# A two-layer denoiser block with an mLSTM layer: the decay rows reach all partitions by DMA and are masked by a select on GpSimd, not by two matmuls a direction, and the written-out orders of the instructions are new

## The chip, the cores and the metric

The kernel runs on one core of one Trainium2 chip. A core has five engines, each with an instruction queue of its own: TensorE (PE in the profile) multiplies matrices, VectorE (DVE) and ScalarE (ACT) work on rows of elements, GpSimd (POOL) does the same and here also starts some transfers, and SyncE (SP) starts most transfers. Each engine works off its queue in order. An instruction that waits for another engine, or for a transfer (DMA), holds up whatever stands behind it on its own queue. SBUF is the memory on the chip with 128 partitions, PSUM the small memory that TensorE writes into.

The metric is the device time of one execution in microseconds (us).

## What is computed

Input are 512 tokens of 1024 features (the latents), 256 tokens of context, and a conditioning vector. Two layers follow one another. Each normalises its tokens, scales and shifts them by the conditioning, mixes them, projects, and adds the result to the tokens with a gate. Layer 0 mixes by a long convolution (hyena) beside attention; layer 1 by an mLSTM, a linear recurrence with 8 heads (key size 128, value size 256) that runs over the tokens forwards and backwards. The change is in layer 1. Its reference, cut to what matters:

```python
def mlstm_chunkwise(q, k, v, i_pre, f_pre, state):        # chunks of the sequence
    def step(carry, inp):
        C, nvec, m = carry
        qc, kc, vc, ic, lfc = inp
        b = jnp.cumsum(lfc, axis=-1)
        d = jnp.where(lower, b[..., :, None] - b[..., None, :] + ic[..., None, :], -jnp.inf)
        inter = b + m[..., None]
        m_row = jnp.maximum(inter, jnp.max(d, axis=-1))
        s = jnp.einsum('bhtd,bhsd->bhts', qc, kc) * jnp.exp(d - m_row[..., None])
        w_prev = jnp.exp(inter - m_row)
        num = jnp.einsum('bhts,bhsv->bhtv', s, vc) + w_prev[..., None] * jnp.einsum('bhvd,bhtd->bhtv', C, qc)
        ...
st_f, hc_f = mlstm_chunkwise(qc, kc, vc, gc[0], gc[1], zero)
_, hl_f = mlstm_chunkwise(ql, kl, vl, gl[0], gl[1], st_f)
...  # and the same with everything flipped, for the backward direction
```

The kernel uses chunks of 128 tokens. With u = i - b and c the running maximum of u (and of the state that enters), the factor exp(d - m_row) for a token t and an earlier token s of the same chunk becomes exp(u[s] - c[t]), and 0 where s comes after t. In the kernel a tile E holds this factor with s along the partitions and t along the row, for the four chunks of the latents side by side: 128 x 512. So E needs, in all 128 partitions, the same row of -c (a row of 512 for each head and direction), a triangle of -1e30 on top of it (the mask), and u[s] as a bias of each partition.

## The kernel before

Everything is in float32, multiplied in pieces: each operand is split into a high and a low part (the function split, L1024: a cast on ScalarE, then a subtraction on VectorE), and a product takes three matmuls (mm3, L1034: high x high, high x low, low x high). Weights come in slices of 1024 x 256 (load_w, L1041): two transfers of 512 KB on SP's queue into tiles wr, each split into a half of a tile wh (ScalarE) and of wl (VectorE). There are 148 such halves. The tokens of a layer, normalised and transposed, lie split in hTh and hTl. Their way there: x_norm (L1144) makes xn, TensorE turns it, h_tile (L1154) scales and splits it.

The order of the instructions is written out by hand, for each part of the kernel. While a part is being recorded (record, L1009), no instruction is issued: an Engine object notes it down. play (L1014) then issues the notes in the order of a list of numbers in the table ORDERS (from L163), and each engine keeps that order. A second table, SLOTS, says for each tag of a pool which of its buffers each new tile takes. There are seven parts: start, hy (hyena), att (attention), out0 (output projection of layer 0 and the first token tiles of layer 1), l1a (first projections and the gates of layer 1), l1b (the eight heads), out1 (output projection of layer 1). Since all instructions are issued by play, the profile gives line L1019 for nearly all of them, and groups are told apart by the names of their tiles.

Layer 1 (from L2209), in the parts that the change and the prediction touch:

- gates (L2228) computes the gates of all heads and both directions at once, rows 0 to 7 forwards and 32 to 39 backwards. It uses ScalarE and VectorE for the most part, with some memsets of POOL ahead of it (gwh, gwl, onesf, gf, gi, q1, q2, zero, ncf, ncs). It leaves cq1 (columns with u and the factors of the keys), cq2, apb, and in ncf the rows of -c. ncf is split into ncs, whose rows 0 to 39 hold the high and rows 64 to 103 the low parts. pick is the sum of two pieces of an identity, so that a column of it, repeated 128 times, picks one row's high and low part and adds them.
- head (L2352) makes keys, queries and values of a head by projections, with short convolutions, then the gates so and zs, and the recurrence (from L2442). psS holds the four products of keys and queries of the chunks. For each direction d the exponent is put together in PSUM by two matmuls of 512 columns: pick's column times ncs writes the row of -c into all 128 partitions, and an identity (identr) times the table mask adds the triangle. ScalarE takes the exponential of it, chunk by chunk, with u as the bias:

```python
TE.matmul(pef, pick[:, col:col + 1].broadcast_to([P, P]), ncs, start=True, stop=False)   # L2452
TE.matmul(pef, identr, mask[:, d], start=False, stop=True)                               # L2453
E = T(mr, "E", (P, 4, P))
for n in range(4):
    S.activation(E[:, n], pe[:, n], AF.Exp, bias=cq1[:, n, col:col + 1])
V.scalar_tensor_tensor(E, psS, QS * KS, E, ALU.mult, ALU.mult)
```

- E is split (Eh, El). The keys, scaled by their factors (ka), are split (kah, kal). For six chunks the state C is updated from a matmul of kah with the values (vh, vl), and num, the result of each chunk, takes a part from Eh and a part from C. Between the steps stand pieces of the projections of so and zs.
- normed divides num by dn, weights it by so, normalises it (hss on ScalarE, hst on VectorE, hrs, a power, on POOL) and multiplies it by zs into hh; result turns hh by TensorE and writes it to DRAM. Both belong to the work left over to the next head. After the last head they stand ahead of out1.

Before the change identr (64 KB) and mask (512 KB) were loaded by POOL's queue at the start of l1a.

Of the kernel before, what the change touches and what calls it, by code (L numbers as in the profile page):

```python
# [7 lines left out]
F32 = mybir.dt.float32  # L8
# [6 lines left out]
P = 128  # L15
# [8 lines left out]
def _hilo(a):  # L24
    """float64 -> two float32 arrays of 12-bit significands whose sum carries 24 bits."""
# [11 lines left out]
def _tables():  # L37
# [8 lines left out]
    s_, t_ = np.arange(P)[:, None], np.arange(P)[None, :]  # L46
    mf = np.where(s_ <= t_, 0.0, -1e30).astype(f32)
    mb = np.where(s_ >= t_, 0.0, -1e30).astype(f32)
    t["mask"] = np.stack([np.tile(mf, (1, 4)), np.tile(mb, (1, 4))], 1)
    # rotary tables  # L50
# [9 lines left out]
    # hyena positional features, decays and transform matrices, tokens ordered phase by phase  # L60
# [27 lines left out]
def _cols(v):  # L88
    """[.., n*128] -> [128, n] columns"""
    v = np.asarray(v)  # L90
    return v.reshape(-1, P).T


def _layout(i):
    """inputs laid out for the device; values unchanged"""
# [58 lines left out]
# columns of vecs  # L154
# [3 lines left out]
class Ctx:  # L158
# [3 lines left out]
# the order in which the instructions noted down in a part of the kernel are issued  # L162
# [2485 lines left out]
```

## Time and profile before

| what | us |
| --- | --- |
| median of 3 runs | 1537.01 |
| lowest and highest of them | 1536.03, 1537.13 |
| span of the profiled execution, first to last instruction | 1533.4 |
| TensorE busy in it | 1499.6 |
| VectorE, ScalarE, GpSimd busy | 988.5, 716.9, 51.7 |

The profiled execution has no total of its own beside its span; the median of the runs is 3.6 us above that span, which is what lies around the first and the last instruction. In the page each engine has its busy time, its share of the span and the number of its instructions. PE's matmuls overlap: the next begins before the one before has ended, so durations of neighbours may not be added. In a row of a timeline stand start, duration, engine, line, operation, the tile written and the tiles read, and in brackets the time for which the engine sat idle before and what ended that. In a row of the list of waits stand the engine and the tile that it was about to write, behind the arrow the engine and tile that it waited for, then the total, the number of times and the longest. In a row of a window stand its length, and for each engine the busy time and in brackets the instructions, then the clock that the throttle granted to TensorE (1.00 is all of it), and the share and rate of the DMA engines.

### The profile page before, as it was taken

Reading aid. Unit: us, or ns where it says so; the run is one execution under the profiler, and the core shown is the slowest. Engines: PE = TensorE matmul, PEld = TensorE weight load, DVE = VectorE, ACT = ScalarE, POOL = GpSimd, SP = SyncE. Lnnn points to the kernel's source line nnn. Section 1 sums busy time; section 2 is a strip of 40 time slices with the busy share of each in tenths; the row PEclk is TensorE's granted clock in tenths of the full one; section 3 lists DMA queues with packets and bytes.
Section 4 is the critical chain, followed back from the end, with each engine's and each line's share of the span. In section 5 each row is a group of like instructions: output and inputs, shape, how many; then the busy total and the mean of one; then the engine's idle time right before and its main releaser. Section 6 shows DMA issues by size and latency. Waiting matters only on the chain.

```text
span 1533.4 us, 26152 instructions
## 1 busy us (share of the span) xinstructions
PE 1499.6 (98%) x10652; PEld 1380.3 (90%) x10652; DVE 988.5 (64%) x1947; ACT 716.9 (47%) x1554; POOL 51.7 (3%) x93
## 2 busy tenths in 40 slices
PE   7999999999999999999999899999999999999997
PEld 4889999889999999989988789999999999999885
DVE  6688786877866666684237755665656565666435
ACT  6643444434435454463225566545545453545332
POOL 1000000000000000000001200000000000000000
PEclk9999999999999999999999999999999999999999
DMA  9421211221130111443442402211221232213741
GB/s 375 138 71 51 78 65 51 71 72 39 40 122 29 38 67 61 156 141 105 175 168 97 147 28 87 67 58 63 97 73 56 73 97 73 70 66 104 257 168 69
DMA packets 42625, 148.13 MB, mean 97 GB/s; under 512 B 4928, under 2 KB 7625, under 8 KB 39946
## 3 DMA queue, kind: packets, MB, share of 16 engines
q1 hardware_dynamic: 38968, 137.12, 25.9%
q0 software_dynamic: 1648, 7.01, 1.4%
q10 hardware_dynamic: 1890, 2.34, 0.5%
q8 instruction: 84, 1.38, 0.3%
q14 instruction: 35, 0.29, 0.1%
HBM read 131.77 MB, written 14.68 MB: 96 GB/s over the span
## 4 chain that ended last, share of the span: by engine, by line
PE 93%; ACT 2%; DVE 2%; issue 1%; DMA 1%; SPq 0%; POOL 0%; POOLq 0%; DVEq 0%; ACTq 0%
PE pj L1019 77%; PE pm L1019 14%; PE s L1019 2%; ACT wh L1019 1%; DMA dfb<-y_scratch 1%; DMA xt<-in_x 0%; DVE wl L1019 0%; DVE hTl L1019 0%; ACT hf L1019 0%; ACT hTh L1019 0%; ACT q L1019 0%; DVE hf L1019 0%; DVE xn L1019 0%; DVE xnT L1019 0%; SPq L1019 0%
## 5 line engine op out<-in xcount | busy, mean ns | idle before, releaser
L1019 PE MATMUL pj<-wh,hTh 128*128 128x256 f32 (+1 forms) x1536 | 442.9, 289 | 3.3 <-ACT wh L1019 3.0
L1019 PE MATMUL pj<-wl,hTh 128*128 128x256 f32 (+1 forms) x1536 | 438.3, 285 | 3.2 <-DVE wl L1019 2.1
L1019 PE MATMUL pj<-wh,hTl 128*128 128x256 f32 (+1 forms) x1536 | 437.8, 285 | 0.0
L1019 PEld LDWEIGHTS pj<-wh,hTh 128*128 128x128 f32 x1536 | 290.0, 189 | 9.4 <-ACT wh L1019 4.3
L1019 PEld LDWEIGHTS pj<-wl,hTh 128*128 128x128 f32 x1536 | 291.5, 190 | 6.6 <-DVE wl L1019 4.3
L1019 PEld LDWEIGHTS pj<-wh,hTl 128*128 128x128 f32 x1536 | 290.9, 189 | 1.4
L1019 PE MATMUL pj<-hTh,wh 128*128 128x512 f32 (+1 forms) x832 | 287.1, 345 | 0.0
L1019 PE MATMUL pj<-hTh,wl 128*128 128x512 f32 (+1 forms) x832 | 285.3, 343 | 0.5 <-DVE wl L1019 0.5
L1019 PE MATMUL pj<-hTl,wh 128*128 128x512 f32 (+1 forms) x832 | 285.3, 343 | 0.5 <-DVE hTl L1019 0.5
L1019 DVE TENSOR_TENSOR wl<-wr,wh 128x1024 fp32r<-128x1024 f32 x148 | 180.1, 1218 | 77.4 <-ACT wh L1019 77.1
L1019 ACT CAST wh<-wr 128x1024 fp32r<-128x1024 f32 x148 | 154.1, 1049 | 72.4 <-PE pj L1019 49.3
L1019 PEld LDWEIGHTS pj<-hTh,wl 128*128 128x128 f32 x832 | 156.7, 188 | 21.2 <-DVE wl L1019 0.9
L1019 PEld LDWEIGHTS pj<-hTh,wh 128*128 128x128 f32 x832 | 156.8, 188 | 19.2 <-issue 0.8
L1019 PEld LDWEIGHTS pj<-hTl,wh 128*128 128x128 f32 x832 | 156.8, 188 | 19.0 <-DVE hTl L1019 0.8
L1019 DVE TENSOR_TENSOR PTl<-pj,PTh 128x384 fp32r<-128x384 f32 (+1 forms) x80 | 40.9, 523 | 21.5 <-ACT PTh L1019 21.4
L1019 ACT CAST PTh<-pj 128x384 fp32r<-128x384 f32 (+1 forms) x80 | 35.1, 459 | 40.9 <-PE pj L1019 38.5
L1019 DVE SCALAR_TENSOR_TENSOR C<-C,apb,pj 128x258 f32<-128x258 f32 x64 | 30.6, 479 | 31.2 <-PE pj L1019 30.2
L1019 DVE TENSOR_TENSOR Cl<-C,Ch 128x258 fp32r<-128x258 f32 x64 | 26.8, 423 | 37.1 <-ACT Ch L1019 36.8
L1019 DVE SCALAR_TENSOR_TENSOR num<-pm,cq,num 128x258 f32<-128x258 f32 x64 | 30.2, 480 | 25.4 <-PE pm L1019 10.9
L1019 PE MATMUL pm<-Rh,dfa 128*128 128x256 f32 (+1 forms) x192 | 44.7, 304 | 0.0
L1019 DVE TENSOR_REDUCE mx<-s 128x1 f32<-128x768 f32 (+1 forms) x48 | 36.9, 771 | 11.2 <-PE s L1019 11.2
L1019 DVE TENSOR_TENSOR med<-big 128x512 f32<-128x512 f32 (+1 forms) x48 | 40.4, 864 | 4.8 <-ACT big L1019 4.6
(341 smaller groups left out, 2725.3 us busy)
## 6 DMA issues: line engine op xcount, KB each, us to landing
wr<-in_o_w_in SPq DMA_DIRECT2D x64, 512.0 KB
wr<-in_e_w_in SPq DMA_DIRECT2D x52, 512.0 KB
wh<-in_w_mod SPq DMA_DIRECT2D x18, 1024.0 KB
wr<-in_e_w_out SPq DMA_DIRECT2D x16, 512.0 KB
wr<-in_o_w_out SPq DMA_DIRECT2D x16, 512.0 KB
xt<-in_x SPq DMA_DIRECT2D x12, 512.0 KB
y_scratch<-y SPq DMA_DIRECT2D x8, 512.0 KB
xt<-in_w_mod SPq DMA_DIRECT2D x6, 512.0 KB
```

The lines of the kernel that those rows point to most:

```text
L1019: x = fn(*a, **k)
```

## The change

The row of -c goes through DRAM. The two blocks of 8 rows of ncf are written to a scratch tensor in DRAM, by two transfers on SP's queue. For each head and direction a transfer on SP's queue reads one row (2 KB) into all 128 partitions of a tile decay (256 KB, two buffers). A select on POOL (affine_select) then puts -1e30 in place of the elements behind the diagonal, for the forward or the backward direction. Exp reads that tile in SBUF. Gone are the 32 matmuls and their 16 tiles of PSUM; the table mask, the loads of mask and identr; ncs with its memset, its split and the tile pick; and the memset of ncf.

```diff
-    identr = T(mg, "identr", (P, P), F32R)
-    G.dma_start(identr, ins["ident"])
-    mask = T(mg, "mask", (P, 2, 512), F32R)
-    G.dma_start(mask, ins["mask"])
...
-    ncs = T(mg, "ncs", (P, NL), F32R)  # rows of -c, high parts and low parts
-    pick = T(mg, "pick", (P, 40), F32R)  # columns that add both parts of a row
+    ncd = nc.dram_tensor("nc_scratch", [2, 8, NL], F32).ap()
...
-        G.memset(f(ncs), 0.0)
-        V.tensor_tensor(pick, ident[:, 0:40], ident[:, 64:104], ALU.add)
         ncf = T(gp, "ncf", (NR, NL))
-        G.memset(ncf, 0.0)
...
-        split(ncs[0:NR], ncs[64:64 + NR], ncf)
+        for d in range(2):
+            SP.dma_start(ncd[d], ncf[32 * d:32 * d + 8])
...
+        decay = []
+        for d in range(2):
+            x = T(mr, "decay", (P, 4, P), bufs=2)
+            SP.dma_start(x, ncd[d, h:h + 1].rearrange("o (n t) -> o n t", n=4).broadcast_to([P, 4, P]))
+            G.affine_select(x, x, [[0, 4], [1 - 2 * d, P]], ALU.is_ge, -1e30, base=0, channel_multiplier=2 * d - 1)
+            decay.append(x)
         psS = PM((P, 4, P))
...
-            pe = PM((P, 4, P))
-            pef = pe.rearrange("p n t -> p (n t)")
-            TE.matmul(pef, pick[:, col:col + 1].broadcast_to([P, P]), ncs, start=True, stop=False)
-            TE.matmul(pef, identr, mask[:, d], start=False, stop=True)
...
-                S.activation(E[:, n], pe[:, n], AF.Exp, bias=cq1[:, n, col:col + 1])
+                S.activation(E[:, n], decay[d][:, n], AF.Exp, bias=cq1[:, n, col:col + 1])
```

The second half of the change are the tables. All lists of ORDERS and most of SLOTS are new, of the parts too whose work stays the same. In "start" each engine keeps its order, and only the order of the issue across engines differs. In hy, att, out0, l1a, l1b and out1 the lists of TensorE, VectorE, ScalarE and SP differ; a TensorE instruction stands on average 22 to 33 places from where it stood, GpSimd's order is nearly as before. In the new lists of TensorE the matmuls of several PSUM tiles alternate more finely, where before a tile's matmuls stood in long runs. The buffers of wr, which were taken in turn (0, 2, 1), are now taken irregularly: 20 times of 148 a half takes the buffer of the half just before it, 14 times before. In l1b the new order has the reads of decay on SP among the loads of weights, and the selects on POOL among the memsets and powers. Comments are gone as well, with no effect on the instructions.

More of the change, by code (lines that the diff above doesn't have):

```diff
@@ L45, in _tables @@
     t["sel"] = sel
[L46 to L49, printed above, removed]
     nf = 32
@@ L808 @@
     "qTh@6": [
-        0, 0, 2, 1, 0, 2, 1, 0, 2,
+        0, 0, 1, 2, 0, 1, 2, 0, 1,
     ],
@@ L869 @@
     "xn@9": [
-        0, 2, 1, 0, 2, 1, 0, 2, 1, 0, 2, 1,
+        0, 1, 1, 2, 0, 2, 1, 0, 2, 1, 0, 1,
     ],
@@ L878 @@
     "cvo@12": [
-        0, 1, 1, 0, 1, 0, 1, 0, 1, 0, 1, 0, 1, 0, 1, 0, 1, 0,
+        0, 1, 0, 1, 1, 0, 0, 1, 1, 0, 1, 0, 0, 1, 0, 1, 1, 0,
     ],
     "vh@12": [
-        0, 1, 0, 1, 0, 1, 0, 1, 0,
+        0, 1, 0, 0, 1, 1, 0, 1, 0,
     ],
     "vl@12": [
-        0, 1, 0, 1, 0, 1, 0, 1, 0,
+        0, 0, 1, 0, 1, 0, 1, 1, 0,
     ],
     "hn@12": [
-        0, 1, 0, 1, 0, 1, 0, 1,
+        0, 1, 0, 1, 0, 0, 1, 0,
+    ],
+    "decay@13": [
+        0, 1, 0, 1, 0, 1, 0, 1, 0, 1, 0, 1, 0, 1, 0, 1,
@@ L907 @@
     ],
     "ess@14": [
-        0, 1, 0, 1,
+        1, 1, 1, 1,
     ],
     "esst@14": [
-        0, 1, 0, 1,
+        1, 0, 1, 0,
     ],
     "ers@14": [
-        0, 1, 0, 1,
+        1, 0, 1, 0,
     ],
     "xt@14": [
-        0, 3, 2, 1,
+        3, 0, 2, 1,
     ],
```

55 lines of the change are left out of this document (29 added, 26 removed), and 1162 rows, old and new, of tables (ORDERS, SLOTS).

## The prediction

> **What bounds the kernel now.** I read the page's first and fourth part first, the engines' busy time and the chain that ended last.
>
> ```profile
> span 1533.4 us, 26152 instructions
> PE 1499.6 (98%) x10652; PEld 1380.3 (90%) x10652; DVE 988.5 (64%) x1947; ACT 716.9 (47%) x1554; POOL 51.7 (3%) x93
> PE 93%; ACT 2%; DVE 2%; issue 1%; DMA 1%; SPq 0%; POOL 0%; POOLq 0%; DVEq 0%; ACTq 0%
> ```
>
> TensorE (PE) is busy 98% of the span, and 93% of the chain is its own work. So a matmul taken away shortens the kernel by its own pace, unless a wait fills the hole. The second view is a table by windows of 20 us: four places where PE is not full, and for comparison one from the middle of the heads (940 to 960).
>
> ```profile
> core 0: us, PE busy (x) PEld busy (x) DVE busy (x) ACT busy (x) POOL busy (x), PEclk, DMA share, GB/s
> 840.00:860.00 20.00, 16.75 (x87) 13.62 (x87) 17.19 (x41) 12.37 (x26) 3.05 (x5) 0.95 0.31 116
> 860.00:880.00 20.00, 17.16 (x106) 15.63 (x106) 16.44 (x27) 10.77 (x22) 8.30 (x17) 0.88 0.54 169
> 900.00:920.00 20.00, 17.69 (x140) 16.55 (x138) 14.63 (x38) 18.71 (x33) 0.00 (x0) 1.00 0.01 2
> 940.00:960.00 20.00, 20.00 (x122) 17.74 (x121) 13.94 (x29) 9.81 (x22) 0.37 (x6) 1.00 0.30 103
> 1420.00:1440.00 20.00, 16.80 (x131) 14.91 (x130) 10.55 (x20) 7.27 (x19) 1.05 (x1) 0.95 0.57 206
> ```
>
> Between 840 and 880, where layer 0's output projection hands tokens to layer 1, PE idles 3.25 + 2.84 = 6.1 us, and the granted clock falls to 0.95 and 0.88: (0.05 + 0.12) x 20 = 3.4 us of clock. 900 to 920 (the gates, ScalarE busy 18.7 of 20) idles 2.3 us; 1420 to 1440 (last head, start of the last projection) idles 3.2 us and loses another 1.0 by its clock. Among the heads PE is busy 20.00 of 20.00. The list of PE's waits says what ended these gaps:
>
> ```profile
> PE pj L1019 <- DMA fw<-in_f_w: 8.0, 1, 8.0
> PE pm L1019 <- DVE xn L1019: 4.1, 4, 1.8
> PE pj L1019 <- ACT wh L1019: 3.0, 3, 1.2
> PE pj L1019 <- DVE wl L1019: 2.5, 5, 0.7
> PE pm L1019 <- DVE hh L1019: 1.2, 1, 1.2
> ```
>
> The 8.0 us are the start and stay. None names a tile of the masks. All waits below the first come to little more than 10 us, so the new orders have little to win and a full PE to spoil.
>
> **Matmuls removed.** The timeline at the first mask of head 0:
>
> ```profile
> 929.61 0.28 PE L1019 MATMUL pj<-vh,kal 128*128 128x258 f32 x1
> 929.72 0.40 PE L1019 MATMUL pm<-ncs,pick 128*128 128x512 f32 x1
> 929.96 0.39 PE L1019 MATMUL pm<-mask,identr 128*128 128x512 f32 x1
> 930.18 0.28 PE L1019 MATMUL pj<-vh,kah 128*128 128x258 f32 x1
> 930.38 0.88 ACT L1019 ACTIVATE E<-pm,cq 128x128 f32<-128x128 f32 x3
> ```
>
> Matmuls overlap, so the price is start to start: 930.18 - 929.72 = 0.46 us for the pair. The groups count the pairs:
>
> ```profile
> L1019 PE MATMUL pm<-ncs,pick 128*128 128x512 f32 x16 | 6.4, 398 | 0.0
> L1019 PE MATMUL pm<-mask,identr 128*128 128x512 f32 x16 | 6.3, 394 | 0.0
> L1019 ACT ACTIVATE E<-pm,cq 128x128 f32<-128x128 f32 x64 | 21.0, 369 | 9.6 <-PE pm L1019 9.4
> ```
>
> 16 x 0.46 = **7.4 us**, all in the full stage, neither matmul with idle time before it. By the durations (6.4 + 6.3) it would be 12.7, which counts the overlap twice. The Trainium skill, "TensorE: Matmul & The Clock Gate", Part 1, puts a 512-column matmul at 215.7 ns start to start, by which the term would be an estimated 6.9; the trace shows 0.23. Exp (0.37 us) now reads SBUF, not PSUM; what that does to its duration falls on an engine that idles half of 940 to 960 (9.81 busy), so nothing of it is on the path.
>
> **Setup removed.** The timeline of GpSimd (POOL) and VectorE (DVE) where the last token tiles are normalised:
>
> ```profile
> 840.61 0.87 DVE L1019 TENSOR_SCALAR xn<-xt,rs 128x512 f32<-128x512 f32 x2
> 865.31 4.08 DVE L1019 TENSOR_SCALAR xn<-xt,rs 128x512 f32<-128x512 f32 x2
> 863.92 0.96 POOL L1019 MEMSET gwh<- 128x1024 f32 x1
> 867.75 0.59 POOL L1019 DMA_DIRECT2D identr<-in_ident  x1
> 868.84 0.67 POOL L1019 DMA_DIRECT2D mask<-in_mask  x1
> 869.50 0.54 POOL L1019 MEMSET ncf<- 40x512 f32 x1
> 868.24 0.63 PE L1019 MATMUL pm<-c_ident,xn 128*128 128x128 f32 x4 [1.80 <-DVE xn L1019]
> ```
>
> The same two operations took 0.87 us elsewhere and 4.08 while POOL ran its block of memsets and DMA issues from 863.9 to 870.0; PE waited 1.80 and then 0.58 us for xn. The change takes identr, mask and ncf out of that block, 1.8 us, but 3.2 us of slowing stays as long as the other memsets do. Gain between 0 and 1.8; I take **1.0**. The split of ncs goes too:
>
> ```profile
> L1019 ACT CAST ncs<-ncf x1: 618/618/618, 919.0 to 919.0; 40x512 fp32r<-40x512 f32 x1
> L1019 DVE TENSOR_TENSOR ncs<-ncf,ncs x1: 687/687/687, 920.3 to 920.3; 40x512 fp32r<-40x512 f32 x1
> L1019 POOL MEMSET ncs<- x1: 528/528/528, 874.6 to 874.6; 128x512 f32 x1
> ```
>
> 0.6 us of ScalarE where it is the busiest, 900 to 920: between 0 and 0.6; I take **0.5**.
>
> **Added: the row by DMA, the select, the wait of Exp.** Sixteen reads of 256 KB, broadcast to 128 partitions, on SP's queue, two small writes, and sixteen selects of 128x512 on POOL. No select is in the trace. The nearest rows:
>
> ```profile
> L1019 POOL TENSOR_TENSOR rq<-qst,mhalf 128x12 f32<-128x12 f32 x5 | 11.4, 2281 | 168.2 <-DVE qst L1019 168.2
> grow<-in_qk_norm POOLq DMA_DIRECT2D x2, 64.0 KB, 3.3
> mask<-in_mask POOLq DMA_DIRECT2D x1, 512.0 KB, 3.8
> identr<-in_ident POOLq DMA_DIRECT2D x1, 64.0 KB, 2.5
> SPq L1019 <- DVE wl L1019: 612.5, 62, 27.1
> L1019 DVE TENSOR_TENSOR wl<-wr,wh 128x1024 fp32r<-128x1024 f32 x148 | 180.1, 1218 | 77.4 <-ACT wh L1019 77.1
> ```
>
> One select costs between 0.53 (the memset of that size) and 2.3 us (the power); one pass over 512 elements, it is nearer to the memset than to a power; I take 1. POOL has 51.7 us of work in all, so 16 to 37 more fit. A read lands in 2.5 to 3.8 us by the DMA rows; 4 MB beside a DMA share of 0.30 fit too.
>
> On time they are by position. In the new order I add the PE work between a head's read on SP and its first Exp, at 0.12 us for a matmul of 256 columns (929.61 to 929.72 above) and 0.23 for 512. For heads 1, 2, 3, 4 and 7, first direction, it comes to 28, 20, 34, 47 and 20 us, for the second directions 21 to 43; need is 3.8 + 2.3 = 6.1. Tight are head 5 (read and Exp at the same point, though the SP instruction before it stands 11 us earlier, so the read may go out up to 11 us early if its buffer is free) and head 6 (its buffer comes free just before). SP waits mostly for wl (row above), so a read behind a blocked wr issue goes late with it. What a late Exp holds is ScalarE's queue: casts of wh and C behind it, and by those DVE's splits and PE. Head 0 has no lead: ncf on ScalarE, write, read, select, Exp in series, 2.5 + 3.3 + 1 = 6.8 us or up to 2.5 + 3.8 + 2.3 = 8.6; in before, ncs was ready at 920.3 + 0.7 = 921.0 and first used at 929.7, 8.7 us of slack. The new order has the first Exp 3 us of PE work earlier, which leaves 8.7 - 3 = 5.7 us for 6.8 to 8.6. So a wait of up to 3 us is possible there and the same at heads 5 and 6, nothing elsewhere: 0 to 9 us, of which ScalarE's own idle time (10 of 20 us in a window) covers most. I take **1.0** lost.
>
> **Orders anew.** The lists of PE, ScalarE, DVE and SP differ in hyena, attention, both projections and layer 1 (PE instructions move 22 to 33 places on average); "start" keeps the order of each engine. The work is the same; what can change are the gaps. Two can be followed:
>
> ```profile
> 1416.40 0.29 PE L1019 MATMUL pm<-Ch,ql 128*128 128x258 f32 x1
> 1424.30 1.56 PE L1019 MATMUL pm<-c_ident,hh 128*128 128x128 f32 x8 [1.25 <-DVE hh L1019]
> ```
>
> At the last head the chain from the last matmuls of num (a run that ends at 1416.5) to the transposes of hh takes 7.9 us, with 5.8 us of PE work in between; the new list puts 7.0 there: **1.2** gained. At the end of layer 0's projection the work between the last token tile's last matmul and its transposes falls from 8.2 to 6.8 us: up to 1.4 lost; I take **0.7**, as the xn gain above is at the same tile. Elsewhere there is little: of PE's idle 33.8 us (1533.4 - 1499.6) the start has 8.0 and the three places above 11.6; the other 14.2, the end of the kernel among them, lie in over 1400 us. I enter nothing and leave it to the range.
>
> Sum: -7.4 - 1.0 - 0.5 - 1.2 + 1.0 + 0.7 = -8.4. On the span: 1533.4 - 8.4 = 1525.0; the median of the runs is 3.6 us above the span, so **1528.6 us**.
>
> **Rivals.** (a) The new orders close the gaps. 6.1 + 3.4 us between 840 and 880, 2.3 at the gates, 4.2 at 1420 to 1440 are 16.0, of which my terms take 2.7 already; two thirds of the rest would be 9 more, about 1520. For it: the same work in better places would do it. Against: chains of ScalarE and DVE, not order alone, set these stages.
>
> (b) Slower: ScalarE's queue stands at Exp. Place: the first Exp of each direction; price: the time by which read and select come late. It decides when the 16 Exps hold PE for over 0.46 us each on average, since that is what a pair returned; at 1 us each the sum has +16 in place of +1.0, so -9.4 + 16 = 6.6 slower, about 1543.6. For it: SP's 612.5 us behind wl, and POOL's queue is in order, so a select behind a norm's power (hrs, which waits for DVE) waits with it. Against: the leads of 20 us and more.
>
> (c) DVE and POOL hold each other up: xn above took 4.08 for 0.87 us beside POOL. If each select held a DVE split by its own 1 to 2.3 us, DVE would lose 16 to 37 us over the 500 us of heads, where it has 6 of 20 idle; that costs PE only where wl (1.2 us a piece) is just in time, and at a tenth of it, 2 to 4 us, the time is about 1532. The Trainium skill, "SBUF — State Buffer", Who interferes with whom, says that a DVE instruction with two SBUF inputs contends with a GpSimd instruction that reads SBUF, not with one that only writes, and that the second fully blocks; by that rule a select, which reads, would hold the splits which are all such two-input forms. The trace has xn, one input, slowed by memsets, a form that the section lists as well; it has no select.
>
> (d) The new order of the full stages (hyena, attention, the heads) adds waits there that eat the matmuls' gain: eight heads with 1 us each are enough, about 1537. Nothing in the profile shows a gap that would grow, but at 98% any gap is new.
>
> (e) The pairs were not on the path: the change gives 0 to 2 us, about 1536. PE's 20.00 of 20.00 in 940 to 960 speaks against it.
>
> **Numbers.** Forecast 0.37 (its own range: all gains at their upper ends and no loss, 1526, to the matmuls alone with losses of 3 + 1.4, 1534); (a) 0.22; (c) 0.10; (d) 0.11 and (e) 0.04; (b) 0.16. A measurement of this kernel tells 0.2%, 3.1 us, from no change. Faster: forecast, (a), (c) and a little of (d), 0.70; same: the rest of (d) and (e), 0.14; slower: (b), 0.16. The range goes from (a) with all of the gaps closed, 1515, to (d) and the milder half of (b), 1541.
>
> **What would show it.** PE's count falls by 32 to 10620 and PE is still at 98%; the 20-us windows of the heads stay at 20.00; no wait named decay in ScalarE's list, or under 3 us in all; select rows on POOL at 0.5 to 2.3 us; hh's 1.25 gone; xn's waits under 4.1 in all; no window of the heads under a clock of 1.00. Wrong if ScalarE waits for decay and PE then for wh or C; if wl grows past 1218 ns on average; if half-clock stretches come or go (the one before 1440 cost 1.0 in its window); or if new waits stand in hyena and attention.

## The result

The changed kernel takes 1569.33 us (median of 4 runs, 1568.98 to 1572.72), the kernel before in the same comparison 1536.55 (1536.03 to 1537.13, 4 runs): a ratio of 1.0221 [1.0207, 1.0236], 32.8 us slower. The prediction said 1528.6 and at most 1541.

The profiled execution of the changed kernel took 1569.42 us with a span of 1567.4, 34.0 more than before. The same three lines of its page:

```profile
span 1567.4 us, 26209 instructions
PE 1523.5 (97%) x10620; PEld 1384.8 (88%) x10620; DVE 1016.4 (65%) x1945; ACT 728.9 (47%) x1553; POOL 60.4 (4%) x105
PE 37%; DVE 3%; ACT 1%; issue 0%; DMA 0%; POOL 0%; POOLq 0%; DVEq 0%; ACTq 0%
```

PE has the 32 matmuls less that were forecast (10620 for 10652) and is busy 23.9 us longer, at 97%. So most of the loss is not idle time: fewer matmuls cover more time. (The shares of the chain here come to 41%: it could not be followed through, and I don't use it.) The windows of 20 us, one from the first part of attention, two from layer 0's projection to layer 1, one of the heads, one at the last head:

```profile
core 0: us, PE busy (x) PEld busy (x) DVE busy (x) ACT busy (x) POOL busy (x), PEclk, DMA share, GB/s
440.00:460.00 20.00, 15.54 (x111) 14.79 (x110) 11.01 (x31) 8.09 (x32) 2.30 (x1) 0.87 0.28 82
880.00:900.00 20.00, 15.70 (x87) 13.40 (x85) 14.91 (x32) 10.92 (x22) 2.51 (x4) 0.83 0.22 78
900.00:920.00 20.00, 14.76 (x82) 13.31 (x83) 13.29 (x21) 8.68 (x18) 5.83 (x12) 0.83 0.43 131
980.00:1000.00 20.00, 20.00 (x125) 17.92 (x125) 15.31 (x32) 10.04 (x21) 0.00 (x0) 1.00 0.36 99
1455.00:1475.00 20.00, 17.44 (x149) 16.22 (x148) 10.08 (x18) 7.62 (x18) 1.01 (x1) 1.00 0.60 218
```

The heads are as full as they were. But 440 to 460, attention, idles 4.46 us at a clock of 0.87, and between 880 and 920 it is 4.30 + 5.24 = 9.5 us at 0.83, where before had 6.1 in its two windows. At the last head, which ends some 35 us later than in before, PE idles 2.56 us for 3.20, and its clock stays full. Both kernels issue a known number of matmuls in each part, so the matmuls can be counted off and the time from a part's first matmul to the next part's first can be read:

| part | before, us | after, us | difference |
| --- | --- | --- | --- |
| start | 43.1 | 43.4 | +0.2 |
| hy | 372.3 | 372.3 | 0.0 |
| att | 314.3 | 342.0 | +27.7 |
| out0 | 137.5 | 149.4 | +11.9 |
| l1a | 48.3 | 50.4 | +2.1 |
| l1b, the heads | 510.9 | 504.1 | -6.9 |
| out1 | 89.0 | 90.2 | +1.2 |

Of the +36 there go 0.5 at the first matmul and 1.9 behind the last one, which leaves the 34.0. The heads, where the masks were, gained 6.9. Attention, which the diff touches only by its order, lost four times as much. Read from the starts of the matmuls, the loss splits as follows. The runs of modulation matmuls, each from its first start to the start of the matmul behind it, take 19.3 us more (att 12.1, out0 5.0, out1 2.2). The matmul just ahead of a run mostly takes 0.2 to 0.3 us to the next start, not 0.12 (0.31 from 562.99 to 563.30 below), and there are 43 runs for 16, so about 4 us more belong to them (an estimate): some 23 in all. PE's idle time ahead of matmuls grows by 11.5 (att 7.4, out0 3.7, l1b 0.4). The removed matmuls give back 7.5, and the rest is mostly the clock: PE runs at half clock for 27.3 us (five stretches, from 454.9, 888.4, 905.5, 939.6 and 949.9), before for 10.2 (6.8 from 857.9 and 3.4 from 1438.2), without the stretch behind the last matmul that each kernel has.

**The modulation.** A modulation row (mod_row, L1107, called in att, out0 and out1) is eight matmuls with an output of 32 partitions each; k-tiles kt and kt + 4 use the same group of 32 columns of the array. In the profile they are the rows pj or pm <- wh,cond of 128*32, two records each. First before, by form, then after:

```profile
L1019 PE MATMUL pm<-wh,cond 128*32 128x256 f32 x160 | 10.7, 385 | 0.0
L1019 PE MATMUL pj<-wh,cond 128*32 128x256 f32 x128 | 8.6, 385 | 0.7 <-DVE dec L1019 0.7
```

```profile
L1021 PE MATMUL pj<-wh,cond 128*32 128x256 f32 x128 | 22.3, 387 | 0.0
L1021 PE MATMUL pm<-wh,cond 128*32 128x256 f32 x160 | 18.5, 386 | 0.2 <-issue 0.2
```

The mean of one is the same, 385 ns before, 387 and 386 after, and the busy time of the two groups grows by 13.7 + 7.8 = 21.5 us. So no matmul is slower, they overlap less. The timeline of PE at such a row, before and after:

```profile
589.41 1.07 PE L1019 MATMUL pj<-wh,cond 128*32 128x256 f32 x16
590.41 0.55 PE L1019 MATMUL pj<-c_ident,hdl 128*128 128x128 f32 x3
```

```profile
562.01 1.05 PE L1021 MATMUL pj<-wh,cond 128*32 128x256 f32 x4
562.99 0.38 PE L1021 MATMUL pj<-wh,hTl 128*128 128x256 f32 x1
563.30 0.62 PE L1021 MATMUL pj<-wh,cond 128*32 128x256 f32 x2
563.86 0.38 PE L1021 MATMUL s<-dfa,qTl 128*128 128x256 f32 x1
564.17 1.05 PE L1021 MATMUL pj<-wh,cond 128*32 128x256 f32 x4
565.15 0.39 PE L1021 MATMUL pj<-wl,hTh 128*128 128x256 f32 x1
```

Before, all 16 records stand in one run and pass in 590.41 - 589.41 = 1.00 us: the four column groups work side by side. After, four records alone take 562.99 - 562.01 = 0.98 us: they are kt and kt + 4 of one group and follow one another. Two records take 563.86 - 563.30 = 0.56. The Trainium skill, "TensorE: Matmul & The Clock Gate", Part 3, says that matmuls with outputs in different groups of 32 columns run at the same time; before's row agrees with it. The runs of both kernels follow one pattern, apart from three that hold a wait and one of 0.46 us: a run in which no group comes twice (1, 2 or 4 matmuls) takes 0.53 to 0.57 us, one in which a group comes twice (2 to 8 matmuls) 0.98 to 1.02. So what counts is into how many runs a row falls. In before each of the 16 rows of these three parts is one run; in after they stand in 2 to 5 runs (att), 1 to 3 (out0), 1 to 4 (out1).

**The waits.** PE's list, the costly rows and the one of hh:

```profile
PE pj L1021 <- DMA fw<-in_f_w: 7.5, 1, 7.5
PE pm L1021 <- ACT hf L1021: 6.0, 4, 2.7
PE pm L1021 <- DVE xn L1021: 4.2, 2, 3.4
PE pj L1021 <- ACT qjunk L1021: 4.2, 4, 2.8
...
PE pm L1021 <- DVE hh L1021: 1.3, 2, 0.8
```

hf and qjunk (the squares that the norm of queries and keys in attention needs) are new among the top rows; nothing here is decay.

### The profile page after: what moved, and what is told of

Read it like the earlier page. It is cut to its first block, busy times and chain, and to the rows that moved or that the text cites. A ratio compares the mean times of both kernels' runs of the same rounds, so it can differ in the third digit from the quotient of the medians.

```text
span 1567.4 us, 26209 instructions
## 1 busy us (share of the span) xinstructions
PE 1523.5 (97%) x10620; PEld 1384.8 (88%) x10620; DVE 1016.4 (65%) x1945; ACT 728.9 (47%) x1553; POOL 60.4 (4%) x105
## 3 DMA queue, kind: packets, MB, share of 16 engines
q1 hardware_dynamic: 41304, 141.35, 27.7%
## 5 line engine op out<-in xcount | busy, mean ns | idle before, releaser
L1021 PE MATMUL pj<-wh,hTh 128*128 128x256 f32 (+1 forms) x1536 | 426.4, 290 | 6.8 <-ACT wh L1021 2.1
L1021 PE MATMUL pj<-wl,hTh 128*128 128x256 f32 (+1 forms) x1536 | 429.7, 289 | 1.3 <-DVE wl L1021 1.3
L1021 PE MATMUL pj<-wh,hTl 128*128 128x256 f32 (+1 forms) x1536 | 426.0, 289 | 0.2 <-DVE hTl L1021 0.2
L1021 PE MATMUL pj<-hTh,wh 128*128 128x512 f32 (+1 forms) x832 | 282.3, 346 | 1.9 <-DVE qTl L1021 1.9
L1021 PE MATMUL pj<-hTl,wh 128*128 128x256 f32 (+1 forms) x832 | 282.7, 344 | 0.6 <-DVE hTl L1021 0.6
L1021 PE MATMUL pj<-hTh,wl 128*128 128x512 f32 (+1 forms) x832 | 280.0, 344 | 0.0
L1021 PE MATMUL s<-dfa,qTh 128*128 128x256 f32 (+1 forms) x160 | 45.8, 341 | 0.0
```

Source lines behind the costliest of these rows:

```text
L1021: x = fn(*a, **k)
```

## The experiments

Two theories to begin with. Mine after the result: the orders of the parts whose work did not change cost the time, first by the broken rows of the modulation, then by waits; the mask's change itself is worth about what was forecast. The rival: DMA reads, selects and what they hold up cost it, in the heads and ahead of them.

### First set: the mask or the orders

The kernel before took 1535.54 us (median of 15 runs) beside these four. **orders_alone** is the kernel before with the new tables:

```diff
-ORDERS = {"start": <before>, "hy": <before>, "att": <before>, "out0": <before>, "l1a": <before>, "l1b": <before>, "out1": <before>}
+ORDERS = {"start": <after>, "hy": <after>, "att": <after>, "out0": <after>, "l1a": <before>, "l1b": <before>, "out1": <after>}
```

> The kernel before (masks by two matmuls), with the new orders and buffers in start, hyena, attention and both output projections, those of before in l1a and l1b. Theory (orders outside layer 1 lose it): attention +28, first projection +12, last one +1: 1575 to 1580 us. Rival (the masks' new way loses it): within 5 us of before.

1578.24 us, 1.0273 [1.0259, 1.0287]. att +27.9, out0 +14.0, out1 +1.2, l1b 0.0. No select and no read of decay is in this kernel, and the loss is all there. The rival falls.

**mask_alone** is the changed kernel with the old tables outside layer 1's middle:

```diff
-ORDERS = {"start": <after>, "hy": <after>, "att": <after>, "out0": <after>, "l1a": <after>, "l1b": <after>, "out1": <after>}
+ORDERS = {"start": <before>, "hy": <before>, "att": <before>, "out0": <before>, "l1a": <after>, "l1b": <after>, "out1": <before>}
```

> The kernel after, with the orders and buffers of before in start, hyena, attention, both output projections; the new orders stay only in the two parts of layer 1 (l1a, l1b). Theory (the new orders outside the heads lost the time, the masks by DMA and select gained their matmuls): attention, output projections and hyena return to their times of before, l1b keeps its -6.9 us, l1a its 2 us or less: 1530 to 1532 us, faster than before by 5 to 7. Rival (reads, selects and the wait of Exp cost the time, directly or by what they do to later parts): still slower than before, 1550 or more.

1536.87, 1.0008 [0.9999, 1.0017]. l1b -8.1 and att -0.4, as my theory has it, but out0 +6.6 (PE's idle time there grows by 4.1 us, with one wait of 2.8 for xn) and l1a +2.1; ahead of l1a's first matmul PE waits 3.4 us for vl. A miss: something ahead of the gates eats the gain even in the old order of out0.

**mod_grouped** is the changed kernel with each row of the modulation put together again, at the place of its last matmul. One row in "att" (its eight matmuls are 1693 to 1700):

```diff
-1704, 1546, 1694, 1696, 1693, 1697, 1695, 1700, 1699, 1705, 1706, 1707, 1698, 1701,
+1704, 1546, 1705, 1706, 1707, 1694, 1696, 1693, 1697, 1695, 1700, 1699, 1698, 1701,
```

> The kernel after, with one thing changed: the eight matmuls of each modulation row (mod_row) in attention and both output projections stand in one run again, at the place of the last of them; after has them in up to 5 runs with other matmuls between. Theory A (broken runs cost pace: the four column groups no longer work side by side): minus 20 to 24 us, about 1547. Theory B (the loss is in waits and the halved clock alone, the order of these matmuls is harmless): no change within 3 us, 1567 to 1571.

1547.9, 1.0076 [1.0063, 1.009], against after 1569.33 - 1547.9 = 21.4 us less. Its groups are back (inside a row the matmuls keep after's order, so that matmuls of one group are still neighbours, and a row takes 1.00 to 1.02 us all the same):

```profile
L318 PE MATMUL pm<-wh,cond 128*32 128x256 f32 x160 | 10.9, 386 | 0.0
L318 PE MATMUL pj<-wh,cond 128*32 128x256 f32 x128 | 8.7, 385 | 0.0
```

**mod_spread2** does the reverse to the kernel before: each of the eight rows in "att" is split into four runs of two, with one other matmul between (here the row is 1365 to 1372, the matmuls between are 1400 to 1402, the other numbers belong to other engines).

```diff
-1400, 1401, 1402, 1365, 1350, 1363, 1345, 1316, 1366, 1367, 1368, 1369, 1356, 1370, 1371, 1372,
+1365, 1366, 1400, 1367, 1368, 1401, 1369, 1370, 1402, 1350, 1363, 1345, 1316, 1356, 1371, 1372,
```

> The kernel before, with one thing changed: in attention each of the eight modulation rows is broken into four runs of two matmuls, with one other matmul between them; nothing else moves by more than three places. Theory A (0.8 us a break, 15 us over 19 breaks in after): 24 breaks, 12 to 19 us slower, 1549 to 1556, all of it in attention, without new waits. Theory B: no change within 3 us.

1550.23, 1.0087 [1.0072, 1.0102]. att +14.0, every other part 0.0, and the waits of PE are those of before (xn 3.9, wh 3.0, wl 2.5). The runs take 9.5 us more, and the 24 matmuls between them take 0.26 to 0.32 us to the next start, not 0.12, about 4 more. Over 8 x 3 = 24 breaks the 14.0 us are 0.6 a break, less than the 0.8 expected:

```profile
L321 PE MATMUL pj<-wh,cond 128*32 128x256 f32 x128 | 20.0, 391 | 0.8 <-DVE dec L321 0.8
```

Taking the breaks out of after moves the time by what the groups show (21.4 us for 21.5). Putting breaks into before moves it by more than the group's busy time (14.0 for 20.0 - 8.6 = 11.4), because the matmuls between the runs take longer to the next start as well. Both go the way of the theory, so this cause is shown, and it is about 21 us.

### Second set: what eats the mask's gain ahead of the heads

Before: 1535.65 (median of 12). In mask_alone PE waited for xn behind the block of memsets that POOL runs ahead of the gates. In after the same place reads, by the timelines of POOL, VectorE and PE, in order of time:

```profile
901.12 0.96 POOL L1021 MEMSET gwh<- 128x1024 f32 x1
...
902.71 4.03 DVE L1021 TENSOR_SCALAR xn<-xt,rs 128x512 f32<-128x512 f32 x2
...
905.98 0.47 POOL L1021 MEMSET zero<- 40x128 f32 x1
906.37 1.75 PE L1021 MATMUL pm<-c_ident,xn 128*128 128x128 f32 x7 [3.36 <-DVE xn L1021]
```

The two halves of xn, 0.87 us elsewhere, last from 902.7 to 906.7, until the block from 901.1 to 906.4 is over, and PE waits 3.36 us. The first half takes 3.60 us, longer than any single memset (0.96). In before the two DMA issues of identr and mask stood inside that block: xn's first half took 2.78 us and ended at 868.09, during the issue of identr (867.75 to 868.34), the second at 869.39, during that of mask (868.84 to 869.51), and PE waited 1.80 and 0.58. Theory: a block of memsets without a gap holds xn for its whole length, so taking the loads out of the block made it worse. Rival: the new order of l1a puts xn late. Three kernels. **mask_l1b** is mask_alone with l1a too in the old order (the removed instructions left out of the list):

```diff
-ORDERS = {..., "out0": <before>, "l1a": <after>, "l1b": <after>, "out1": <before>}
+ORDERS = {..., "out0": <before>, "l1a": <before>, "l1b": <after>, "out1": <before>}
```

> The masks by DMA and select, with the orders and buffers of before everywhere but in l1b; l1a has the order of before too, without what the change removes and with the two writes of the rows behind ncf. It differs from mask_alone only in l1a. Theory (the 6 us that mask_alone lost between the two layers come from the new order of l1a and of POOL's memsets): l1b -8, the end of out0 and l1a within 2 us of before, 1528 to 1531. Rival (they come from the change itself, which takes identr, mask and ncf out of POOL's block): out0 and l1a still 4 us or more above before, 1533 to 1537.

1528.9, 0.9957 [0.9945, 0.997]. l1a +0.2 instead of +2.1, l1b -8.2, out0 +2.6, a little over the 2 expected, att +1.3. (The +1.3 is one wait for dec in the profiled execution; mask_hold has the same order of att and -0.6 there.) So the new order of l1a cost most of what mask_alone lost; but xn still takes 4.35 us (its first half 3.95, up to 870.07, with the block's end at 869.79), and PE waits 5.8 for it in all, 4.8 of them at once, more than before's 4.1. **mask_hold** adds one small copy on POOL ahead of the block, which reads the last token tile's hTh and so starts the memsets only when that tile is through:

```diff
+    hold = T(mg, "hold", (P, 1))
+    G.tensor_copy(hold, f(hTh[:, KT - 1, 3 * P:3 * P + 1]))
```

> mask_l1b with one instruction more: POOL first copies one column of the last token tile's hTh, so its block of memsets starts only when the last tokens are normalised, turned and scaled. Theory (a DVE tensor_scalar cannot run while POOL's memsets hold the port; in before the two DMA issues between them let the two halves of xn through, without those issues xn waits for the whole block): xn takes 0.9 us a pair in place of 4.1 to 4.3, PE's waits for xn fall below 1.5 us, and with them a stretch of halved clock: 3 to 6 us faster than mask_l1b. Rival (xn's duration there has another cause, or the block costs as much later): within 1.5 us of mask_l1b.

1524.7, 0.9933 [0.992, 0.9945], the fastest kernel of this study: 10.9 us under before, 44.6 under the changed kernel. The same timelines:

```profile
864.60 0.87 DVE L318 TENSOR_SCALAR xn<-xt,rs 128x512 f32<-128x512 f32 x2
...
865.75 1.03 PE L318 MATMUL pm<-c_ident,xn 128*128 128x128 f32 x8
...
869.74 0.70 POOL L318 COPY hold<-hTh 128x1 f32<-128x1 f32 x1 [6.48 <-ACT hTh L318]
870.39 0.95 POOL L318 MEMSET gwh<- 128x1024 f32 x1
```

With the block out of the way xn is back at 0.87 us and the transposes start without a wait for it. In all PE still waits 2.2 us for xn, more than the 1.5 expected. **before_hold** is the kernel before with the same two lines:

```diff
+    hold = T(mg, "hold", (P, 1))
+    G.tensor_copy(hold, f(hTh[:, KT - 1, 3 * P:3 * P + 1]))
```

> The kernel before (masks by matmuls) with the same one copy ahead of POOL's block of memsets. Theory of the port: xn's waits of PE fall from 4.1 to about 1.7 us, and the halved clock near 858 gets shorter or stays: 2 to 5 us faster than before. Rival: within 1.5 us of before, or slower because the gates' weights come later.

1531.37, 0.9973 [0.9963, 0.9984]. xn 0.87, PE's waits for it 2.2 in all in place of 4.1; out0 -3.0 and l1a +1.1. So the block cost the kernel before 4 us too. That memsets hold xn is shown. The Trainium skill, "SBUF — State Buffer", Who interferes with whom, names tensor_scalar among the forms of DVE that can contend with GpSimd, with the other side blocked for a whole instruction; the trace agrees that it is held (4.03 and 4.35 for 0.87), but here over several memsets in a row, not over one instruction. That it was the two DMA issues that opened a gap in before is argued from the times only; no run moved them alone.

**mask_hand** asks whether the new order of the heads has a part in their gain: mask_l1b with l1b in the old order as well, without the 32 matmuls, each read of decay right behind the last Exp of the same direction in the previous head, each select behind its read.

```diff
-ORDERS = {..., "l1a": <before>, "l1b": <after>, "out1": <before>}
+ORDERS = {..., "l1a": <before>, "l1b": <before, reads and selects put in>, "out1": <before>}
```

> mask_l1b, but l1b too in the order of before, without the 32 matmuls; each read stands right behind the last Exp of the same direction of the head before, each select behind its read. Theory (the gain is the removed matmuls, the order of l1b matters little): l1b -6.5 to -7.5, within 1.5 us of mask_l1b. Rival (the order of l1b makes the gain, and a read on SP's queue behind weights that wait comes late): l1b above -4, ScalarE waiting for decay.

1530.66, 0.9966 [0.9952, 0.998]. l1b -4.6 in place of -8.2, which neither side expected, and 1.8 us above mask_l1b where the theory allowed 1.5. No wait of ScalarE names decay, but the reads cost something in another way. At head 0, by the timelines of SP, ScalarE and PE:

```profile
923.07 0.82 SPq L318 DMA_DIRECT2D decay<-nc_scratch  x2
923.98 0.85 SPq L318 DMA_DIRECT2D wr<-in_o_w_in  x2
931.02 1.04 ACT L318 CAST wh<-wr 128x1024 fp32r<-128x1024 f32 x1 [3.92 <-DMA wr<-in_o_w_in]
933.63 0.39 PE L318 MATMUL pj<-wh,hTh 128*128 128x256 f32 x1 [2.33 <-ACT C L318]
```

Both reads stand ahead of the next weights on SP's queue, so these go out at 923.98, in before at 920.14. ScalarE then waits 3.92 us for the weights, the copy C stands behind them, and PE waits 2.33 us for it. In mask_l1b one issue of weights goes out between the two reads (923.32). No run moved the reads alone, and the intervals of the ratios of mask_hand and mask_l1b overlap; how much the new order of l1b is worth of its own is not settled.

### Third set: the select, and a theory on attention that fell

Before: 1535.67 (median of 7). **select3** is mask_hold with every select done three times (the same values come out):

```diff
-            G.affine_select(x, x, [[0, 4], [1 - 2 * d, P]], ALU.is_ge, -1e30, base=0, channel_multiplier=2 * d - 1)
+            for _ in range(3):
+                G.affine_select(x, x, [[0, 4], [1 - 2 * d, P]], ALU.is_ge, -1e30, base=0, channel_multiplier=2 * d - 1)
```

> mask_hold with each of the 16 selects done three times over (the result is the same). A select took 0.64 us in after; 32 more are 20 us of GpSimd beside the heads. Theory (selects cost nothing on the path; neither GpSimd's time nor a lock of the port reaches TensorE): within 1.5 us of mask_hold, VectorE's splits Cl, El, wl within 3% of their means. Rival (a select and a VectorE instruction with two SBUF inputs shut each other out): splits in the heads visibly longer, up to 0.6 us for each that meets a select, l1b 2 us or more slower.

1524.92, 0.9928 [0.9912, 0.9945], l1b 503.5 for 503.7 us. The row of the select (count, then min/median/max in ns, first and last start):

```profile
L318 POOL TENSOR_SCALAR_AFFINE_SELECT decay<-decay x48: 636/638/1504, 921.2 to 1343.5; 128x512 f32<-128x512 f32 x48
```

32 more selects cost nothing on the time. VectorE's splits hardly change on average (means in mask_hold and here: Cl 438 and 442 ns, wl 1219 and 1223, El 688, kal 820), because few of them meet a select. Those that do are another matter. The splits Cl in before, where there is no select, and one of them in after:

```profile
L1019 DVE TENSOR_TENSOR Cl<-C,Ch x64: 395/422/430, 933.4 to 1415.7; 128x258 fp32r<-128x258 f32 x64
```

```profile
977.35 0.63 POOL L1021 TENSOR_SCALAR_AFFINE_SELECT decay<-decay 128x512 f32<-128x512 f32 x1 [9.18 <-ACT Ch L1021]
977.38 0.88 DVE L1021 TENSOR_TENSOR Cl<-C,Ch 128x258 fp32r<-128x258 f32 x1 [0.24 <-ACT Ch L1021]
```

This split starts 0.03 us behind a select and takes 0.88 us for 0.42. In select3 one wl that starts behind a select takes up to 1656 ns for 1218, and a select that starts behind a split up to 1504 for 636. So a select and a two-input instruction of VectorE do hold each other: the one that starts second is stretched until the other is nearly through. By the rule of the Trainium skill that the prediction cited, a select, which reads SBUF, and a split with two inputs exclude one another; the single instances agree. The rival was right about the splits and the theory about the time: both engines have room for it.

**att_grouped** went for the rest of attention's loss. There PE changes from one PSUM tile to another 734 times in the new order, 245 in the old. It is mod_grouped with all matmuls of a PSUM tile of "att" in one run, at the place of the last. Some of these matmuls then read operands that later steps have already rewritten, so it computes something else in attention; only its times are used.

```diff
-"att": [<mod_grouped>]
+"att": [<mod_grouped, the matmuls of each PSUM tile together at the place of the last>]
```

> mod_grouped with one more change, in attention alone: all matmuls of a PSUM tile stand in one run, at the place of the tile's last one (TensorE changes from tile to tile 245 times there, as in before, not 734 times as in after), and each tile takes the buffer that has been free longest. Orders of ScalarE and VectorE stay those of after. Theory (of the 14.6 us by which attention is still above before in mod_grouped, most come from accumulators that stay open while others are worked on, so that buffers of PSUM come free just before they are needed: 12 instructions of slack in the middle case, 23 in before, 37 here): attention 315 to 320 us, 1534 to 1539. Rival (the orders of ScalarE and VectorE make the waits): attention stays above 325, 1545 to 1549.

1577.16, 1.0267 [1.0252, 1.0282]; att 359.4 us, 45.1 over before; PE idles about 30 us more there, and 20.5 us of it pass at half clock, none in before. The theory of the open PSUM tiles fell: putting the matmuls together late makes more waits than it removes.

### Fourth set: the squares of attention

Before: 1535.95 (median of 7). In after ScalarE's queue stands for 23.4 us in front of squares (qjunk) that are placed behind VectorE's first use of the same tile. **att_qfirst** is mod_grouped with the two squares of 25 such tiles moved ahead of VectorE's first read (41 below; the squares are 39 and 40):

```diff
-36, 37, 38, 41, 85, 86, 87, 88, 7, 60, 61, 8, ..., 98, 42, 39, 40, 135,
+36, 37, 38, 39, 40, 41, 85, 86, 87, 88, 7, 60, 61, 8, ..., 98, 42, 135,
```

> mod_grouped with one more change, in attention: in 25 of 30 PSUM tiles of queries and keys ScalarE's two squares (qjunk) stand ahead of VectorE's first reading of the tile again, as they do in before in all 30; after lets the two engines take turns. Theory (two engines that read a PSUM tile do so one after the other, in the order of the list; turns back and forth keep the tile, and TensorE waits for its buffer): ScalarE's waits of qjunk for VectorE (29 us there, none in before) go, PE's waits for qjunk, rt and qTl (8.2 us) mostly too, and the halved clock near 457 and 477 with them: 6 to 10 us faster than mod_grouped, 1538 to 1542. Rival (the waits come from where the weights' casts and splits stand on those queues): within 2 us of mod_grouped.

1548.43, 1.0086 [1.0069, 1.0103], mod_grouped's time again. In ScalarE's list only one row of qjunk is left, and it names PE:

```profile
ACT qjunk L318 <- PE pj L318: 30.9, 13, 6.6
```

PE's 4.2 us for qjunk are gone too, and att stays at 328.5: waits for hdh (2.0), rt (2.1), qTl (1.9), dec (1.3) and PTh (1.2) have come in their place. That theory fell as well.

**after_mended** is att_qfirst with the copy hold of mask_hold:

```diff
+    hold = T(mg, "hold", (P, 1))
+    G.tensor_copy(hold, f(hTh[:, KT - 1, 3 * P:3 * P + 1]))
```

> att_qfirst with the copy ahead of POOL's block of memsets that mask_hold has. Theory (three separate faults of the new orders): a further 3 to 6 us, from PE's wait of 3.4 us for xn and the halved clock after it: 1533 to 1538. What is left above mask_hold is then the order of the first projection (hf) and of l1a. Rival: the wait moves to the next instruction and less than 1.5 us is gained.

1544.97, 1.0057 [1.0042, 1.0072]: 3.5 less than att_qfirst; out0 falls from 143.1 to 138.7, PE's waits for xn from 4.1 to 1.0. The gain is as expected, the time is not (1533 to 1538 was expected), since att_qfirst, from which it starts, had missed. Its waits for hf, 6.3, stay.

### Fifth set: where in attention

Before: 1535.57 (median of 13). Open was which stretch of attention's new order waits. **att_head_old** is mod_grouped with the first 776 of the 3143 instructions of "att" in before's order, as far as before comes by 500 us, and the others in after's, **att_tail_old** the reverse, after's order up to 520 us and before's behind it:

```diff
-"att": [<mod_grouped>]
+"att": [<before: the first 776>, <mod_grouped: the others>]
```

```diff
-"att": [<mod_grouped>]
+"att": [<mod_grouped: the first 850>, <before: the others>]
```

> mod_grouped, but the first quarter of attention (keys and first queries, as far as before had come at 500 us) stands in the order of before, and the rest in that of after; buffers by which has been free longest. Theory (the 14 us that neither the modulation rows nor the order of the squares explain lie in the stretch of 420 to 480 us, where after has most of PE's idle time): attention falls from 329 to 318 to 321 us, 1537 to 1540 in all. Rival (they are spread over the whole of attention, a little at each switch between tiles): half or more stays, 1541 or more.

> The other half: mod_grouped with the order of after up to 520 us and that of before for the rest of attention. Theory (the loss lies at its start): attention stays at 325 us or more, 1544 to 1549. Rival (spread): it falls to 320 us or less, 1540 or less.

att_head_old: 1538.23 (1535.57 to 1543.03, 10 runs, a wide spread; the profiled one took 1540.49, with out0 10.0 over before for mod_grouped's 5.5), 1.0019 [1.0008, 1.003]; att 317.6, 3.3 over before in place of mod_grouped's 14.6. att_tail_old: 1546.62, 1.0064 [1.0047, 1.008]; att 326.0, still 11.6 over before. The window of before, which was not shown yet, and of att_head_old:

```profile
core 0: us, PE busy (x) PEld busy (x) DVE busy (x) ACT busy (x) POOL busy (x), PEclk, DMA share, GB/s
440.00:460.00 20.00, 20.00 (x168) 19.84 (x167) 12.13 (x35) 9.61 (x38) 2.31 (x1) 1.00 0.25 93
```

```profile
440.00:460.00 20.00, 20.00 (x167) 19.69 (x166) 12.13 (x35) 9.79 (x38) 2.31 (x1) 1.00 0.29 92
```

With before's order there PE is full again at full clock, where after had 15.54 and 0.87. So 11.3 of the 14.6 us that attention loses beside the modulation lie in the stretch up to 500 us, and PE's idle time there is mostly between 420 and 480; 3.3 remain behind it.

## Why the prediction was wrong

The step that failed is "Orders anew": "The work is the same; what can change are the gaps", and for all parts but two places "I enter nothing and leave it to the range". Both halves were wrong.

- **The same work does not take the same time.** The eight matmuls of a modulation row share about 1 us as long as they stand in one run. Broken up they cost about 21 us (mod_grouped -21.4, mod_spread2 +14.0 for att alone), without a gap. It could have been seen beforehand: the row of 16 records in 1.07 us stood in the trace, and that the new lists tear a tile's matmuls apart stood in the description of the change. I followed positions of reads and tiles, not the runs that are fast for being runs.
- **Gaps that did not exist can open.** PE was full from 440 to 460 in before and idles 4.46 us there in after. The first stretch of attention, up to 500 us, costs some 9 to 11 us (1547.9 to 1538.23; att +14.6 to +3.3). I read "little to win" from a full PE and drew no size for what could be lost. Rival (d) named new waits in hyena, attention and the heads, but priced them by the heads, at 8 us, so the range ended at 1541. Hyena's new order cost nothing (372.3 us in both), and the heads gained.

The other terms:

- **Matmuls removed, -7.4.** Right: mask_hold and mask_l1b gain 7.2 and 8.2 in l1b, after 6.9, with 7.5 at the places of the removed matmuls; mask_hand gains 4.6, with a new wait of 2.3 us for C.
- **The added chain, +1.0, and the select, 1 us.** ScalarE's list has no row for decay, so rival (b) and head 0's wait fell for this kernel. mask_hand shows another form of it: with both reads ahead of the weights on SP, ScalarE waits for the weights. A select takes 0.64 us and a read lands in 4.0, a little above the 3.8 that I took as the upper end. In the page's groups and DMA issues, and in the list by operation:

```profile
L1021 ACT ACTIVATE E<-decay,cq 128x128 f32<-128x128 f32 x64 | 24.7, 398 | 0.8 <-DVE El L1021 0.8
```

```profile
L1021 POOL TENSOR_SCALAR_AFFINE_SELECT decay<-decay x16: 634/636/918, 963.4 to 1387.7; 128x512 f32<-128x512 f32 x16
```

```profile
decay<-nc_scratch SPq DMA_DIRECT2D x16, 256.0 KB, 4.0
```

  Exp is slower from SBUF, 398 for 369 ns, on an engine with room, as said.
- **xn, -1.0.** Wrong in sign: PE waits 5.8 us for xn in mask_l1b and 5.0 in mask_hand, 4.1 in before, and out0 is 2.6 and 0.4 longer. I took the 1.8 us out of the block and left the gap out of account that they seem to have made in it. Moving the whole block brought 4.2 us to this kernel (1528.9 to 1524.7).
- **ncs, -0.5.** Not separable: l1a's parts differ by +0.2 in mask_l1b and -0.3 in mask_hold.
- **hh, -1.2.** It did not come: at the last head the wait is 0.84 us for 1.25, and a head before it has a new one of 0.49. I counted the work between by positions of PE and left out ScalarE, VectorE and POOL, whose lists changed as well.
- **Last token tile, +0.7.** out0 lost 11.9: about 6 by the modulation (an estimate from its runs, 5.0, and the matmuls ahead of them), 3.7 in waits (xn and hf), most of the rest by the clock.
- **From the span to the time, +3.6.** Too large. It set the median beside the span of a faster execution; wherever one execution has both figures, here, they lie about 2 us apart (2.0 to 2.1 in after, 1.7 to 1.9 in before).
- **Rivals.** (a) fell: no gap closed, that of the last head shrank from 3.20 to 2.56 us. Of (c) the mechanism is there, since single splits are held, but its price on the time is nothing (select3). (e) fell by l1b. The sum without the orders was fair: mask_l1b, which is the change without the new tables outside the heads, takes 1528.9. But that hides +2.6 in out0 and +1.3 in att against the -8.2, and the 3.6 for about 2, so the agreement is partly luck and no proof of each term.

What stays open: which instructions of attention's first stretch make the waits (not the rows of the modulation, not the squares alone, and not open PSUM tiles alone); the 6 us of waits for hf at layer 1's first projections, which come with after's order of out0 (orders_alone has 5.9 with the old l1a, mask_alone 0.5 with the new one); and the 2 us that the new order of l1a costs in l1a. Within a part the lists of the engines depend on one another, so the old list of one engine with the new of the others was not tried.

## What to carry to other kernels

When an order is rewritten, first list the runs of instructions that are fast only together (matmuls in different column groups, one row of 16 records in 1.00 us here) and see that the new order keeps them; a count and a mean duration show nothing of it, the busy time of the group does. At 98% busy a new order has little to win and much to lose (43 us here), so its range belongs far to the slow side, and a change of the work is best timed with the old order first: here that separates the mask's -7 us (mask_l1b) from the +43 of the orders (orders_alone). And a block of memsets has a place too: hold it until what VectorE does beside it is through.

## What the runs showed of the hardware

- Matmuls of 32 output partitions in four column groups: a run takes 0.53 to 0.57 us when no group comes twice in it and 0.98 to 1.02 when one does, eight matmuls at most. Each break by one other matmul costs 0.6 us (mod_spread2). Neighbours of one group inside a whole row cost nothing (1.00 to 1.02 us in mod_grouped).
- A run of memsets on POOL with no gap held two fp32 tensor_scalars of VectorE for nearly the whole block, 4.03 to 4.35 us for 0.87. A select of 128x512 on POOL (0.636 us) and a two-input instruction of VectorE hold each other: the second one is stretched (Cl 0.88 us for 0.42, wl 1.66 for 1.22, the select up to 1.50). Few meet, and it cost no time here, even with the selects tripled.
- PE runs at half clock in stretches of 3.4 or 6.8 us, 27.3 us in the changed kernel and 10.2 before. Most stand in or right behind places where PE waits, the one at 939.6 in after does not, and before's at 857.9 lies ahead of its wait for xn at 868.2. mask_hold still has that one and select3, with the same code there, has not, so they come and go between executions; no run changed the clock alone.
